# Crossbar turns of the first two mLSTM heads: the loads that turn them on ScalarE's queue, the head's norm ahead of the next scores

## The chip, the cores and the metric

The kernel runs on one core of a Trainium2 chip. The metric is device time in microseconds (us). The core's engines are named as the profile names them: PE (TensorE, matrix products), DVE (VectorE), ACT (ScalarE), POOL (GpSimd) and SP (SyncE, which here does nothing but issue DMAs). DMAs are issued by SP, POOL or ACT and carried out by 16 DMA engines that they share. Each engine takes its instructions in the order in which they were written out; an instruction that waits holds all that stand behind it on that engine.

## The reference, cut to what matters

A trunk of two layers over 256 latent tokens and 256 context tokens, width 1024. Layer 0 mixes tokens by an mLSTM with four heads, then comes a ConvFFN; layer 1 is a latent attention with eight heads, then a ConvFFN. The change lies in the mLSTM alone, whose heads are computed so:

```python
q, k = jnp.split(x_c @ w_qk, 2, axis=-1)          # per head: 256 columns of q, 256 of k
v = (x_m @ w_v)                                    # per head: 512 columns
wmat = jnp.exp(dmat - mj[..., None]) * jnp.einsum("bhjd,bhsd->bhjs", qc, kc)
num = ... + jnp.einsum("bhjs,bhse->bhje", wmat, vc)
h = num / jnp.maximum(jnp.abs(den), jnp.exp(-mj))[..., None]
...
o = jax.nn.sigmoid(h_in @ w_og)                    # output gate
hsum = o * s
return _head_rms_norm(hsum, norm_g) @ w_out        # a norm over each head's 512 columns
```

The kernel does not scan in chunks: for each head it forms the whole 512 x 512 matrix of decays and scores, for both directions.

## The kernel before, in words

**Products.** A product in fp32 is done as three matmuls on a high and a low part (`mm3`, L428: L431, L434, L435). `split` (L444) makes the two parts: a cast on ACT (L445) gives the high one, a subtraction on DVE (L446) the low one.

**Weights.** `Stream` brings weights in tiles of 128 x 1024 (512 KB, tile `raw`) on SP's queue (L309), three of them ahead. Each is split as well: the cast of `w` or `wu` on ACT (L346), the low part on DVE (L369). A `raw` tile is free for the next load when both have read it. One tile feeds 24 matmuls of 128 x 512.

**The loop over heads** (`build`, L2250 on). For each head h PE does, in this order: 192 matmuls `qk` (`w_qk`, 8 weight tiles), then for h of 1 and more the 36 matmuls `av` of the head before (`av`, L1169), then the 24 matmuls `sc` and `sl` of this head's scores (`s_mm`), which ACT copies to `S` (L1043). `w_qk` takes two steps of the background (`bg`) after each of its eight weight tiles, sixteen in all, and what a step writes stands on every engine at that place. Ahead of its seventh tile it calls `v_load` for the head before: loads of `vr` and `oh` on POOL (L1139, L1145) and the split of `v`.

**What is in the background of `w_qk(h)`.** `head(h-1)`: the decays `aB` are loaded on POOL (L1051) and masked on DVE (`Am`, L1056), the exponentials of `W` are made on ACT (L1093), `W` is multiplied by the scores, summed and divided on DVE (L1094 to L1111), turned on PE (`PT`, L1124: 12 matmuls of 128 x 128) and split. For h of 2 and 3 also `post(h-2)`, the norm of the head before that: sums of squares on ACT (`jk`, L1194), a root with a table load (L1195), a reciprocal and a scaling on DVE (L1196, L1198); that is its first step. Its second step turns the rows into two planes of 16 bits (`pl`, ACT, L450) and stores them to DRAM on POOL (`hd`, L1205). They come back turned by four loads through the DMA's crossbar (`turn_load`, L1246, DMA_TRANSPOSE, on SP's queue), and `turn_split` splits them to `hn` on ACT and DVE (L1254, L1255). `mixed` (L1225) deals these out over the sixteen steps by a string: `h` is a step of `head`, `p` one of `post`, `L` a turning load, `S` a `turn_split`, `.` nothing.

**Beside it** runs the modulation of later layers (`ada_bg`): 1.2-us products on DVE (`junk`, L550), each of which reads a one-element gate that ACT copies just before (`adav<-w` or `mod<-w`, L565); their loads `ar` are on SP (L573). POOL also prepares sums of weights for later (`t4d`, L1709).

**After the loop** come the matmuls `y` of the output projection, with `head(3)`, `post(2)` and the `v` of head 3 in the background; their `W` is turned by the same line L1124.

Of the kernel before, what the change touches and what calls it, by code (L numbers as in the profile page):

```python
# [10 lines left out]
U16 = mybir.dt.uint16  # L11
# [390 lines left out]
class K:  # L402
# [620 lines left out]
    def s_mm(self, h):  # L1023
# [10 lines left out]
        for jb in range(2):  # L1034
# [4 lines left out]
            pl.append(p)  # L1039
        S = []  # L1040
        for p in [pc] + pl:
            s = self.s2("S")
            nc.scalar.activation(s, p, AF.Copy, scale=1.0 / 16.0)  # L1043
            S.append(s)
        return S

    def head(self, h, S, big=False):
        nc = self.nc
# [13 lines left out]
        for g in range(3):  # L1062
# [9 lines left out]
            for i, t in enumerate(jbs):  # L1072
                base = 256 * i if g == 0 else 0
                for d in range(2):
# [17 lines left out]
                    for s0, s1, src in spans:  # L1092
                        nc.scalar.activation(o[:, base + s0:base + s1], src[:, s0:s1], AF.Exp, bias=bias, scale=1.0)  # L1093
                    nc.vector.scalar_tensor_tensor(o[:, base + lo:base + hi], o[:, base + lo:base + hi], 1.0,  # L1094
                                                   S[g][:, base + lo:base + hi], op0=ALU.mult, op1=ALU.mult,
                                                   accum_out=den[:, 2 * i + d:2 * i + d + 1])
# [127 lines left out]

    def mixed(self, head, post):  # L1225

        plan = "h p p hp h hL . L hL . hLS h S S . S"
        for step in plan.split():
            for op in step:
                if op in "hp":  # L1230
                    next(head if op == "h" else post, None)
                elif op == "L":
                    self.turn_load()
                elif op == "S":
                    self.turn_split()
            yield

    def turn_load(self):

        h, d, e = self.turned[0]  # L1240
        if e == 3:
            self.turned.pop(0)
        else:
            self.turned[0] = h, d, e + 1
        x = self.s2("hx")
        self.nc.sync.dma_start_transpose(x.bitcast(U16), d.rearrange("t h n -> (t h) n")[:, e * 128:(e + 1) * 128])  # L1246
        self.hx.append((h * 4 + e, x))

    def turn_split(self):
# [979 lines left out]
def build(tc, off, a, out):  # L2229
    es = ExitStack()  # L2230
    with es:
        k = K(tc, es, off, a)
# [14 lines left out]
        S = None  # L2247
        tt = None
        k.hn, k.turned, k.hx = {}, [], []
        for h in range(H0):  # L2250
            gens = []
            if h == 0:
                gens.append(k.gate_chain())
            if h >= 2:
                gens.append(k.mixed(k.head(h - 1, S), k.post(h - 2, tt)))
            elif h >= 1:
                gens.append(k.head(h - 1, S))
            k.bg = gens
            k.w_qk(h, 2, (lambda: k.v_load(h - 1)) if h >= 1 else None)
            k.drain()  # L2260
            if h >= 1:
                tt = k.av(h - 1)
            S = k.s_mm(h)
        k.xc = None
        hn = lambda i: (k.hn[i][:, 0], k.hn[i][:, 1])
# [7 lines left out]
        tt = k.av(3)  # L2273
# [136 lines left out]
```

## Time and profile before

| | us |
|---|---|
| three runs | 1359.21, 1360.93, 1361.62 (median 1360.93) |
| the profiled execution | 1360.79 |
| its span, from first to last instruction | 1359.0 |
| PE busy | 1337.2 |
| DVE busy | 1058.1 |
| ACT busy | 718.3 |
| POOL busy | 146.1 |

The span is what the trace shows; 1.79 us of the profiled execution lie around it. Busy time of PE is the time in which a matmul is in flight; its mean granted clock is 0.993 of full speed. In a timeline a row is an instruction or a run of equal ones: start, duration, engine, line, what it writes and reads, and in brackets how long the engine stood idle before it and whose end released it. Durations of matmuls overlap, so their cost is the distance from start to start, 0.227 us for a 128 x 512 one at full clock.

### The profile page before, as it was taken

To read this page: it belongs to the slowest core of one execution; us is meant where nothing else is said; L and a number is where in the kernel's file an instruction comes from. 1 tells how busy PE (TensorE), PEld (TensorE's weight loads), DVE (VectorE), ACT (ScalarE), POOL (GpSimd) and SP (SyncE) were. 2 spreads that over 40 slices of the span, in tenths; PEclk is the share of its full clock that TensorE was granted. 3 is DMA by queue.
4 is the path that set the end of the run, shared out by engine and by line. 5 is a ranking of instruction groups with operands and counts; after the bars stand their busy time and mean duration, and the time that the engine had idled before them with its cause. 6 is when DMAs were issued, how large, how long until landed. Compare 5 with 4: busy or idle time off the path is not lost.

```text
span 1359.0 us, 18747 instructions
## 1 busy us (share of the span) xinstructions
PE 1337.2 (98%) x6627; PEld 1120.7 (82%) x6627; DVE 1058.1 (78%) x1745; ACT 718.3 (53%) x1260; POOL 146.1 (11%) x244
## 2 busy tenths in 40 slices
PE   9999999999999999889999999999999999999997
PEld 5777888888888878768898888888888988988886
DVE  4798656677788578787979987857889888898873
ACT  4765443455734456365644343333566768566660
POOL 0222000011201011120002111112000002000100
PEclk9999999999999999889999999999999999999999
DMA  9988847789676386966728989967976537466760
GB/s 363 325 277 275 277 170 235 246 287 300 224 269 221 135 217 210 251 242 231 235 76 283 290 275 296 265 183 186 311 233 187 162 102 213 143 205 191 258 191 32
DMA packets 108975, 308.24 MB, mean 227 GB/s; under 512 B 20888, under 2 KB 33688, under 8 KB 108800
## 3 DMA queue, kind: packets, MB, share of 16 engines
q1 hardware_dynamic: 71440, 220.75, 48.9%
q0 software_dynamic: 26640, 68.84, 18.6%
q10 hardware_dynamic: 10800, 17.44, 3.7%
q8 instruction: 52, 0.85, 0.2%
q14 instruction: 43, 0.35, 0.1%
HBM read 272.21 MB, written 44.21 MB: 233 GB/s over the span
## 4 chain that ended last, share of the span: by engine, by line
PE 92%; DMA 3%; DVE 2%; SPq 1%; issue 1%; ACT 1%; DVEq 0%; ACTq 0%
PE fin L1550 8%; PE y L435 6%; PE y L434 6%; PE y L431 6%; PE tok L431 6%; PE tok L434 6%; PE tok L435 6%; PE fin L434 6%; PE fin L431 6%; PE fin L435 6%; PE qk L431 3%; PE qk L435 3%; PE qk L434 3%; DMA raw<-in_ws 3%; PE up L724 2%; PE up L431 1%
## 5 line engine op out<-in xcount | busy, mean ns | idle before, releaser
L369 DVE TENSOR_TENSOR w<-raw,w 128x1024 fp32r<-128x1024 f32 (+2 forms) x286 | 342.8, 1202 | 153.7 <-ACT w L346 153.2
L346 ACT CAST w<-raw 128x1024 fp32r<-128x1024 f32 (+2 forms) x286 | 296.2, 1037 | 299.7 <-PE tok L435 77.3
L550 DVE SCALAR_TENSOR_TENSOR junk<-ar,bc 128x1024 f32<-128x1024 f32 x128 | 155.8, 1217 | 5.4 <-DMA raw<-in_ws 2.1
L434 PE MATMUL fin<-h,w 128*128 128x512 f32 (+1 forms) x370 | 139.6, 377 | 0.0
L431 PE MATMUL fin<-h,w 128*128 128x512 f32 (+1 forms) x370 | 139.5, 377 | 0.0
L435 PE MATMUL fin<-h,w 128*128 128x512 f32 (+1 forms) x370 | 139.3, 377 | 0.0
L1550 PE MATMUL fin<-h,w 128*128 128x512 f32 (+1 forms) x636 | 111.1, 337 | 0.0
L1550 PEld LDWEIGHTS fin<-h,w 128*128 128x128 f32 x636 | 97.6, 190 | 13.2
L431 PE MATMUL qk<-xc,w 128*128 128x512 f32 x256 | 100.0, 391 | 0.0
L435 PE MATMUL qk<-xc,w 128*128 128x512 f32 x256 | 99.7, 390 | 0.0
L434 PE MATMUL qk<-xc,w 128*128 128x512 f32 x256 | 99.6, 389 | 0.0
L435 PEld LDWEIGHTS fin<-h,w 128*128 128x128 f32 x370 | 69.6, 188 | 12.9
L434 PEld LDWEIGHTS fin<-h,w 128*128 128x128 f32 x370 | 69.6, 188 | 12.8
L431 PEld LDWEIGHTS fin<-h,w 128*128 128x128 f32 x370 | 69.6, 188 | 12.7
L435 PEld LDWEIGHTS qk<-xc,w 128*128 128x128 f32 x256 | 48.0, 188 | 10.0
L431 PEld LDWEIGHTS qk<-xc,w 128*128 128x128 f32 x256 | 48.1, 188 | 9.9
L434 PEld LDWEIGHTS qk<-xc,w 128*128 128x128 f32 x256 | 48.1, 188 | 9.9
L431 PE MATMUL tok<-w,hT 128*128 128x512 f32 x128 | 49.9, 390 | 0.0
L434 PE MATMUL tok<-w,hT 128*128 128x512 f32 x128 | 49.8, 389 | 0.0
L435 PE MATMUL tok<-w,hT 128*128 128x512 f32 x128 | 49.8, 389 | 0.0
L741 ACT ACTIVATE fg<-fg 128x512 f32<-128x512 f32 (+1 forms) x44 | 23.1, 525 | 50.0 <-DVE fg L739 43.9
L369 DVE TENSOR_TENSOR wu<-raw,wu 128x1024 fp32r<-128x1024 f32 (+1 forms) x37 | 44.0, 1204 | 7.0 <-ACT wu L346 6.5
(490 smaller groups left out, 3139.1 us busy)
## 6 DMA issues: line engine op xcount, KB each, us to landing
raw<-in_ws SPq DMA_DIRECT2D x282, 512.0 KB, 4.6
ar<-in_adaT SPq DMA_DIRECT2D x80, 512.0 KB, 5.6
t4d<-in_ws POOLq DMA_DIRECT2D x20, 512.0 KB, 8.7
adaw<-in_ada SPq DMA_DIRECT2D x16, 512.0 KB, 8.2
zr<-fd ACTq DMA_DIRECT2D x33, 128.0 KB, 4.4
xmd<-xr POOLq DMA_DIRECT2D x16, 256.0 KB, 4.6
xcd<-cv POOLq DMA_DIRECT2D x16, 256.0 KB, 5.1
xs<-xmd POOLq DMA_DIRECT2D x16, 256.0 KB, 6.9
```

The source lines that it names most:

```text
L346: self.cast = k.nc.scalar.copy(h[:, :cols], src)
L369: i = self.k.nc.vector.tensor_sub(l[:, :n], src, h[:, :n])
L431: q = mm(out, w[0], x[0], start=start, stop=False, skip_group_check=on)
L434: mm(out, w[0], x[1], start=False, stop=False, skip_group_check=on)
L435: mm(out, w[1], x[0], start=False, stop=stop, skip_group_check=on)
L550: nc.vector.scalar_tensor_tensor(o, w, 1.0, self.bc[j], op0=ALU.mult, op1=ALU.mult, accum_out=col[:, k, j:j + 1])
L724: nc.tensor.matmul(ps[m], wk[i][:, c], hT[k][:, j], start=made[m] == 0, stop=made[m] == 23)
L741: nc.scalar.activation(tmp[:, :n], tmp[:, :n], AF.Silu)
L1550: self.nc.tensor.matmul(ps[:, 0:256] if x else ps, w[x][:, k * 128:(k + 1) * 128], h[:, 0:256] if x else h, start=i == 0 and not k0, stop= ...
```

## The change

Three edits, all in the mLSTM.

```diff
     def mixed(self, head, post):
 
-        plan = "h p p hp h hL . L hL . hLS h S S . S"
+        plan = "p hp h hL h hL . L hS L hS . S . S ."
...
-        self.nc.sync.dma_start_transpose(x.bitcast(U16), d.rearrange("t h n -> (t h) n")[:, e * 128:(e + 1) * 128])
+        self.nc.scalar.dma_start_transpose(x.bitcast(U16), d.rearrange("t h n -> (t h) n")[:, e * 128:(e + 1) * 128])
...
             if h >= 2:
-                gens.append(k.mixed(k.head(h - 1, S), k.post(h - 2, tt)))
+                gens.append(k.mixed(k.head(h - 1, S), post))
...
             if h >= 1:
                 tt = k.av(h - 1)
+                if h < 3:
+                    post = k.post(h - 1, tt)
+                    next(post)
             S = k.s_mm(h)
```

The turning loads go from SP's queue to ACT's. The norm of heads 0 and 1 is written right behind their `av`, ahead of the next scores, and no longer inside the next `w_qk`. The plan puts the planes and stores first, the steps of `head` at 2, 3, 4, 5, 6, 9 and 11 (before at 1, 4, 5, 6, 9, 11 and 12), the turning loads at 4, 6, 8 and 10 (before 6, 8, 9 and 11) and the splits of the turned tiles at 9, 11, 13 and 15 (before 11, 13, 14 and 16). On PE the 12 turns `PT` of heads 1 and 2 so stand behind 120 of the 192 `qk` matmuls where they stood behind 144. On POOL the stores `hd` and the loads `aB` change places: two `hd`, one `aB`, two `hd`, one `aB`, where both `aB` stood first; the `t4d` stand behind them in place of between.

The first place is ACT in the middle of the third head's `qk`. Before, its instructions from the last four exponentials of `W` up to the gate copies of the modulation are these:

```order
L1093 ACTIVATE W<-Am_3915,gcol 128x128
L1093 ACTIVATE W<-aB_3909,gcol 128x384
L1093 ACTIVATE W<-Am_3916,gcol 128x128
L1093 ACTIVATE W<-aB_3910,gcol 128x256
L346 CAST w<-raw 128x1024
L445 CAST qk<-qk 128x512
L346 CAST w<-raw 128x1024
L565 COPY adav<-w 1x1 x5
```

And now, with the turning loads among them (the first of the four stands three rows ahead of these, before the cast of `qk` and that of a weight tile):

```order
L1093 ACTIVATE W<-Am_3940,gcol 128x128
L1093 ACTIVATE W<-aB_3934,gcol 128x384
L1093 ACTIVATE W<-Am_3941,gcol 128x128
L1093 ACTIVATE W<-aB_3935,gcol 128x256
L1246 DMA_TRANSPOSE hx<-hd 128x1024
L346 CAST w<-raw 128x1024
L1246 DMA_TRANSPOSE hx<-hd 128x1024 x2
L565 COPY adav<-w 1x1 x3
L445 CAST qk<-qk 128x512
```

Three turning loads now stand between the last exponential and the gate copies that release the modulation's products on DVE.

The second place is DVE just then, at the end of the same head's `W`. Before, a part of a weight tile stands ahead of the last product of `W`, the one that `PT` reads:

```order
L1104 RECIPROCAL R<-R 128x2
L550 SCALAR_TENSOR_TENSOR junk,adav<-ar,bc 128x1024
L1109 TENSOR_SCALAR W<-W,R 128x512
L369 TENSOR_TENSOR w<-raw,w 128x1024
L1111 SCALAR_TENSOR_TENSOR W<-W,R 128x512
```

And now a product of the modulation does:

```order
L1104 RECIPROCAL R<-R 128x2
L1109 TENSOR_SCALAR W<-W,R 128x512
L550 SCALAR_TENSOR_TENSOR junk,adav<-ar,bc 128x1024
L1111 SCALAR_TENSOR_TENSOR W<-W,R 128x512
L446 TENSOR_TENSOR qk<-qk 128x512
```

That product reads a gate copy of L565, which stands behind the third and fourth turning load on ACT: the last row of `W` now comes after them.

The third place is ACT behind `PT`, ahead of the `av` of the same head. Before:

```order
L346 CAST w<-raw 128x1024
L445 CAST PT<-PT 128x512 x3
L1254 ACTIVATE hn<-hx,sm 128x512
L445 CAST qk<-qk 128x512
L445 CAST v<-vr 128x512 x4
L1254 ACTIVATE hn<-hx,sm 128x512 x3
L346 CAST w<-raw 128x1024
```

And now:

```order
L346 CAST w<-raw 128x1024
L445 CAST PT<-PT 128x512 x3
L1254 ACTIVATE hn<-hx,sm 128x512 x2
L565 COPY adav<-w 1x1
L445 CAST qk<-qk 128x512
L445 CAST v<-vr 128x512 x4
L346 CAST w<-raw 128x1024
```

The rows read alike, but `PT` now comes one weight tile earlier: the cast at the top of the first list and the one at the foot of the second are of the same weight tile (108 casts of L346 stand up to it in either program), and the casts of `PT` and `v` no longer stand behind it.

## The prediction

> **What bounds the kernel now.** The page first: PE is busy nearly the whole span.
>
> ```profile
> PE 1337.2 (98%) x6627; PEld 1120.7 (82%) x6627; DVE 1058.1 (78%) x1745; ACT 718.3 (53%) x1260; POOL 146.1 (11%) x244
> ```
>
> So the change, which adds and removes no matmul, can win only where PE waits or runs below its full clock. The waits of PE come next (what waited, for what, total, times, longest):
>
> ```profile
> PE PT L1124 <- DVE W L1111: 5.4, 1, 5.4
> PE av L431 <- ACT v L445: 2.7, 1, 2.7
> PE av L434 <- DVE v L446: 2.4, 2, 1.3
> ```
>
> All three are in the mLSTM. PE's timeline says what they cost, measured over whole stretches. The 36 `av` and 24 score matmuls run from the first `av` to the next first `qk` (head 0), the next first `qk` (head 1), and the first `y` (head 2):
>
> ```profile
> 446.71 0.39 PE L431 MATMUL av<-v,PT 128*128 128x512 f32 x1
> ...
> 459.05 0.39 PE L431 MATMUL qk<-xc,w 128*128 128x512 f32 x1
> ...
> 503.93 0.40 PE L431 MATMUL av<-v,PT 128*128 128x512 f32 x1
> ...
> 518.43 0.39 PE L431 MATMUL qk<-xc,w 128*128 128x512 f32 x1
> ...
> 563.07 0.39 PE L435 MATMUL qk<-xc,w 128*128 128x512 f32 x1
> 566.19 0.80 PE L431 MATMUL av<-v,PT 128*128 128x512 f32 x1 [2.74 <-ACT v L445]
> ...
> 582.43 0.39 PE L431 MATMUL y<-w,hn 128*128 128x512 f32 x1
> ...
> 592.18 0.39 PE L434 MATMUL y<-wu,hn 128*128 128x512 f32 x1
> 597.95 1.12 PE L1124 MATMUL PT<-ident,W 128*128 128x128 f32 x4 [5.38 <-DVE W L1111]
> ```
>
> Head 0 is undisturbed: 12.34 us (48 matmuls 512 wide at the pitch of 0.227 and 12 of `sc` at half of it would be 12.2). Head 1 takes 14.50, **2.16** more. Head 2 should start at 563.07 + 0.23 = 563.30 and takes 19.13, **6.79** more. The transposes of head 3 come at 597.95 where 592.18 + 0.23 = 592.41 was due, **5.54** late. Behind two of the three places the clock is down (windows: start and end, length, busy time and count of each engine, granted clock, DMA share, GB/s):
>
> ```profile
> 596.50:603.40 6.90, 5.45 (x15) 4.50 (x16) 6.90 (x23) 6.40 (x16) 0.00 (x0) 0.51 0.16 67
> 565.80:572.70 6.90, 5.46 (x12) 4.00 (x13) 6.90 (x12) 6.90 (x12) 1.07 (x2) 0.51 0.97 349
> ```
>
> The second lies in the 6.79 already. In the first, 5.45 us of work at 0.51 cost 5.45 x 0.49 = **2.7**. Together 2.16 + 6.79 + 5.54 + 2.7 = 17.2 us that can go.
>
> What released `v` so late? ACT's timeline for heads 1 and 2 and the chain of waits:
>
> ```profile
> 499.64 1.05 ACT L346 CAST w<-raw 128x1024 fp32r<-128x1024 f32 x1 [11.87 <-DMA raw<-in_ws]
> 500.60 1.56 ACT L445 CAST PT<-PT 128x512 fp32r<-128x512 f32 x3
> ...
> 503.12 2.20 ACT L445 CAST v<-vr 128x512 fp32r<-128x512 f32 x4
> ...
> 562.02 1.05 ACT L346 CAST w<-raw 128x1024 fp32r<-128x1024 f32 x1 [14.77 <-DMA raw<-in_ws]
> ...
> 565.49 2.20 ACT L445 CAST v<-vr 128x512 fp32r<-128x512 f32 x4
> ```
> ```profile
> 486.69 12.85 DMA raw<-in_ws
> ```
>
> ACT stood 11.87 and 14.77 us at a weight cast with `PT`, `qk` and `v` queued behind it. The load it waited for was issued at 486.69, behind turning loads on SP, and needed 12.85 us. SP's own timeline shows how long turning loads hold their issuer:
>
> ```profile
> 476.90 1.25 SPq L1246 DMA_TRANSPOSE hx<-hd  x1
> ...
> 480.36 6.23 SPq L1246 DMA_TRANSPOSE hx<-hd  x3
> ...
> 540.27 9.21 SPq L1246 DMA_TRANSPOSE hx<-hd  x3
> ```
>
> **The change part by part.** (1) *Turning loads off SP's queue.* For SP they go altogether: in that stretch it issues weight and modulation loads only. The load that went out at 486.69 can go out once its buffer is free, up to 6.2 us sooner, and its fellow a head later up to 9.2. I don't count on it landing sooner, though: the median from issue to landing in this stretch is that of a crowded bus, on queues that never had a turning load too:
>
> ```profile
> raw<-in_ws SPq DMA_DIRECT2D x6, 512.0 KB, 12.8
> ...
> vr<-vd POOLq DMA_DIRECT2D x4, 256.0 KB, 7.0
> oh<-od POOLq DMA_DIRECT2D x4, 256.0 KB, 11.8
> aB<-ad POOLq DMA_DIRECT2D x2, 256.0 KB, 5.1
> ```
>
> The Trainium skill speaks against this part: "DMA: Bandwidth & Descriptors", section "Issuing engines are not separate DMA queues", holds that issuing from several engines saves only the time of the issuing sequencer, since the same 16 DMA engines carry it all. The 7.0 and 11.8 us on POOL's queue agree with it; by that rule alone the weight would land as late as before, and the sum would stay at 1347 by part (2) or, without it, at 1361.
>
> (2) *The plan.* PT and the `v` casts move ahead of the cast that was late. Even if its load lands at 499.5 again, `v` no longer stands behind it. I estimate the `v` casts from `PT`: at 24 matmuls earlier, 491.69 (the row below) less 24 x 0.227 = 5.44, PE reaches `PT` at 486.25; three casts (1.56), two `hn`, one `qk` and four `v` (2.20) then end on ACT by about 496 (the estimate allows `hn` and `qk` as much as `v`), DVE's shares a microsecond later, against `av` due at 503.9. Some 6 us of slack: 2.16 and 6.79 go. The loads `vr` stand behind `W` in the old order and in the new, so they go out earlier with it.
>
> ```profile
> 491.69 1.47 PE L1124 MATMUL PT<-ident,W 128*128 128x128 f32 x12
> ```
>
> (3) *PT 5.44 us earlier* needs `W` that much earlier. Before, its last product ran at 490.15 (below), 15.6 us from the second batch of exponentials at 475.32 to its end at 490.89. That batch waited for the second table load, behind the planes:
>
> ```profile
> 470.11 3.89 ACT L450 COPY pl<-oh 128x1024 uint16<-128x1024 uint16 x4 [1.97 <-DVE oh L1198]
> 474.02 1.28 ACT L1093 ACT_TABLE_LOAD   x1
> 475.32 0.69 ACT L1093 ACTIVATE W<-Am,gcol 128x128 f32<-128x128 f32 x2
> ...
> 477.09 0.57 ACT L445 CAST qk<-qk 128x512 fp32r<-128x512 f32 x1
> ...
> 478.51 0.40 ACT L1093 ACTIVATE W<-Am,gcol 128x128 f32<-128x128 f32 x1
> ...
> 480.49 0.61 ACT L1093 ACTIVATE W<-aB,gcol 128x384 f32<-128x384 f32 x1
> ```
> ```profile
> 455.06 0.69 DVE L1184 TENSOR_TENSOR oh<-av,oh 128x512 f32<-128x512 f32 x1 [2.03 <-PE av L435]
> ...
> 469.59 1.68 DVE L1198 TENSOR_SCALAR oh<-oh,ss 128x512 f32<-128x512 f32 x4
> ...
> 490.15 0.74 DVE L1111 SCALAR_TENSOR_TENSOR W<-W,R 128x512 f32<-128x512 f32 x1
> ```
>
> *The norm first* moves all this: the outputs are complete at 455.75; the last square sum, a score copy, a table load (1.28) and the root end near 458.9 (estimated from the rows of the same kinds), the scaling (1.68) near 460.8, planes (3.89) 463.9. One weight cast and the second table load follow: the exponentials may start at 467.3, or once `aB`, now issued among and behind the stores at 463 to 465, has landed, 5.1 us later, by 470. I take the middle, 468.6, against 475.32. From there ACT needs 3.5 us for eleven exponentials (six took 1.77, from 475.32 to 477.09; five others are partly wider), 1.25 for the first turning load, 1.4 for the casts of `qk` and a weight (477.09 to 478.51), 1.5 for four exponentials, two of them wide (0.61): 7.6 in all.
>
> Now the new dependence: the last product of `W` stands behind a modulation product whose gate copy stands behind turning loads 2 to 4 on ACT. The trace of before has no turning load on ACT. Lower bound: 3 x 1.25 = 3.8 us, each as the single one on SP; upper bound: 9.2, the three at 540.27. I take the 6.2 at 480.36, which is the same stretch. With one cast (1.05), the modulation product (1.2) and the last product of `W` (0.74): 468.6 + 7.6 + 6.2 + 3.0 = **485.4**, against PE's arrival at 486.25: a slack of 0.9 us, with `aB` and the turning loads able to move it by 3 either way. I book 0.5 per head, 1.0 for the two.
>
> The norm ahead of the scores also delays ACT's `S` copies by about 1 us; the exponentials that follow start no earlier than 467.3, which hides it. The stores on POOL go earlier by the same 7 us, so the turning loads find their data.
>
> (4) *Head 3's PT*, 5.54 + 2.7. Its exponentials need `S`, which ACT copied behind a late weight, and DVE had no idle time from the stall at 562.02 to the first `y`:
>
> ```profile
> 584.55 1.05 ACT L346 CAST wu<-raw 128x1024 fp32r<-128x1024 f32 x1 [5.41 <-DMA raw<-in_ws]
> ```
> ```profile
> 563.10:582.40 19.30, 15.51 (x62) 12.24 (x61) 19.30 (x28) 11.15 (x20) 2.13 (x4) 0.82 0.84 287
> ```
>
> The scores end about 582.4 and `S` could follow only at 584.55 + 0.96 = 585.5, so without that wait it comes 3.1 us earlier; a mere shift leaves 5.5 - 3.1 = 2.4 late. DVE without its backlog may take the rest. Bounds: nothing stays, or all 8.2. I take 2.0 lost, clock included.
>
> **Sum:** 17.2 - 1.0 - 2.0 = 14.2. The profiled execution of 1360.79 becomes 1346.6; the median of the runs is 0.14 above it: **1347**.
>
> **The rivals.** *PT waits for W behind the turning loads on ScalarE.* If these hold ACT 9.2 us as at 540.27, `W` is ready at 488.4, a wait of 2.1 us, and a wait of 2.74 was followed by half clock at 566.19: another 2.7. Two heads lose 9.6; with the 1.0 booked taken out of the 1346.6, that is 1345.6 + 9.6 = 1355, and 1358 if `aB` lands at 470. For it: four loads in one queue behind each other, now beside SP's weight loads. Against: they are spread over six steps and find an empty queue.
>
> *Nothing gained: the loads move, the bus stays.* If the weights land as late and something else in the queue ahead of `v` waits for them (the cast just before `PT`, which now stands a tile earlier but whose `raw` may be a late one as well), the waits of `av` and of head 3 stay: about 1361. For it: 12.8 us for a load in this stretch. Against: the load ahead of that one was cast at 486.49 in time, and the late one now stands behind `v`. (The rule of the Trainium skill cited above would have the loads as late as this rival has them.)
>
> *Slower: the turning loads hold ACT longer than they held SP.* One mechanism, at the second to fourth of them. Beside it 17.2 - 2.0 = 15.2 us are won, so it decides when each head loses 7.6, a wait of 4.9 and 2.7 of clock: at a hold of 6.2 + 0.9 + 4.9 = 12.0 us. At twice the 9.2 of 540.27, 18.4, the wait would be 11.3, two heads would lose 28, and 1345.6 + 28 = 1374. For it: weight loads that stood still behind the turning loads now run against them on the same DMA engines. Against: nothing in the trace holds an issuer that long.
>
> **How the numbers follow.** Forecast 0.60, from 1343.5 (nothing given back) to 1349.5. PT waiting for W 0.18, 1350 to 1358. Nothing gained 0.10. Slower 0.12. A measurement of this kernel tells about 0.2%, 2.7 us, from no change: faster 0.78, same 0.10, slower 0.12. The range runs from 1343 to 1360: it holds the forecast, the first rival and a little of the second.
>
> **What would show it right or wrong.** Right: no `av` row with a wait; SP's weight loads go out without gaps while ACT shows four DMA_TRANSPOSE of 1 to 3 us; `PT` of heads 1 and 2 unwaited or under a microsecond; the wait at head 3 below 2 us with full clock. Wrong in (3): a wait of PT for W in heads 1 and 2 and half clock behind it. Wrong in (2): ACT idle for `raw` ahead of `PT`. Wrong in all: turning loads of more than 4 us each on ACT.

## The result and the profile after

| | before | after |
|---|---|---|
| first runs, median (lowest to highest), us | 1361.18 (1359.21 to 1361.62, 4 runs) | 1347.49 (1344.9 to 1349.55, 4 runs) |
| ratio to before, 95% interval | | 0.9901 [0.9878, 0.9924] |
| the profiled execution, us | 1360.79 | 1349.55 |
| its span, us | 1359.0 | 1347.8 |

The kernel became faster by 13.7 us, 1.0%. Five more runs of the changed kernel, made later beside the last experiments, had a median of 1344.72 (1343.19 to 1348.15).

The waits of PE after, in the same view as before (what waited, for what, total, times, longest); both waits of `av` are gone; of `PT` one is left and a small one has come (the second row stood there before, too):

```profile
PE PT L1124 <- DVE W L1111: 4.6, 2, 4.2
PE idle L661 <- DVE adav L503: 1.5, 1, 1.5
```

PE's timeline at the same places, the `av` and score stretches of heads 1 and 2 and `PT` of heads 2 and 3:

```profile
503.67 0.39 PE L431 MATMUL av<-v,PT 128*128 128x512 f32 x1
...
516.01 0.39 PE L431 MATMUL qk<-xc,w 128*128 128x512 f32 x1
...
544.25 0.52 PE L1124 MATMUL PT<-ident,W 128*128 128x128 f32 x3 [0.41 <-DVE W L1111]
...
561.51 0.39 PE L431 MATMUL av<-v,PT 128*128 128x512 f32 x1
...
573.86 0.39 PE L431 MATMUL y<-w,hn 128*128 128x512 f32 x1
...
582.01 0.39 PE L431 MATMUL y<-wu,hn 128*128 128x512 f32 x1
586.59 1.12 PE L1124 MATMUL PT<-ident,W 128*128 128x128 f32 x4 [4.19 <-DVE W L1111]
```

Head 1 now takes 516.01 - 503.67 = 12.34 us and head 2 takes 12.35, as head 0 did before: the 2.16 and 6.79 are won whole. `PT` of head 3 comes at 586.59 where 582.01 + 0.23 = 582.24 was due: still 4.35 late, against 5.54. Behind it the clock is down for a shorter time than before (windows; busy time of PE 3.21, granted clock 0.55):

```profile
586.00:589.80 3.80, 3.21 (x10) 2.73 (x11) 3.77 (x15) 3.80 (x8) 0.00 (x0) 0.55 0.48 189
```

That costs 3.21 x 0.45 = 1.4 in place of 2.7. The balance of this execution: 2.16 + 6.79 + (5.54 - 4.35) + (2.7 - 1.4) - 0.41 = 11.0 us, of 1359.0 - 1347.8 = 11.2.

ACT's timeline in head 1's stretch holds the first surprise. `ACTq` is the part of ACT that issues; `ACT` the part that computes:

```profile
471.51 0.40 ACT L1093 ACTIVATE W<-Am,gcol 128x128 f32<-128x128 f32 x1 [4.00 <-DVE Am L1056]
471.67 1.47 ACTq L1246 DMA_TRANSPOSE hx<-hd  x1
...
473.28 0.50 ACT L1093 ACTIVATE W<-aB,gcol 128x256 f32<-128x256 f32 x1
473.35 2.57 ACTq L1246 DMA_TRANSPOSE hx<-hd  x1
473.68 0.39 ACT L1093 ACTIVATE W<-Am,gcol 128x128 f32<-128x128 f32 x1
...
476.03 1.25 ACTq L1246 DMA_TRANSPOSE hx<-hd  x1
...
477.37 1.26 ACTq L1246 DMA_TRANSPOSE hx<-hd  x1
477.59 1.03 ACT L346 CAST w<-raw 128x1024 fp32r<-128x1024 f32 x1
478.68 0.38 ACT L565 COPY adav<-w 1x1 f32<-1x1 f32 x3
```

The issue at 473.35 takes 2.57 us, and exponentials and casts that stand ahead of it in the program run meanwhile without a gap: a turning load is issued while the work written ahead of it is still being computed. It holds only what stands behind it, and only when that earlier work runs out first. The same in head 2's stretch:

```profile
533.65 5.64 ACTq L1246 DMA_TRANSPOSE hx<-hd  x1
533.91 0.56 ACT L445 CAST qk<-qk 128x512 fp32r<-128x512 f32 x1
...
539.39 1.26 ACTq L1246 DMA_TRANSPOSE hx<-hd  x1
540.69 0.38 ACT L565 COPY mod<-w 1x1 f32<-1x1 f32 x3 [2.83 <-DVE R L1100]
```

Of an issue of 5.64 us and one of 1.26, ACT stood idle 2.83 (the releaser named, a DVE instruction, is not what the copy stood behind: it runs as the last issue ends).

The second surprise is in the issues (KB each, median us from issue to landing), in the stretch where a weight took 12.8, `oh` 11.8 and a turning load 14.5 us before:

```profile
raw<-in_ws SPq DMA_DIRECT2D x8, 512.0 KB, 6.7
...
vr<-vd POOLq DMA_DIRECT2D x4, 256.0 KB, 5.4
oh<-od POOLq DMA_DIRECT2D x4, 256.0 KB, 7.5
hx<-hd ACTq DMA_TRANSPOSE x4, 6.6
```

All of these land sooner, the weights in about half the time, and the weight cast that had waited 11.87 us runs at 495.56 without a wait. The prediction had not counted on that. Which of the three edits did it?

### The profile page after: what moved, and what is told of

It is laid out like the page before. It is cut to its first block, busy times and chain, and to the rows that moved or that the text cites. A ratio compares the mean times of both kernels' runs of the same rounds, so it can differ in the third digit from the quotient of the medians.

```text
span 1347.8 us, 18731 instructions
## 1 busy us (share of the span) xinstructions
PE 1332.8 (99%) x6627; PEld 1118.6 (83%) x6627; DVE 1059.7 (79%) x1745; ACT 719.8 (53%) x1260; POOL 146.7 (11%) x244
## 4 chain that ended last, share of the span: by engine, by line
PE 82%; issue 10%; DVE 4%; DMA 2%; POOL 1%; ACT 1%; DVEq 0%; SPq 0%; POOLq 0%; ACTq 0%
PE fin L1550 8%; PE y L434 6%; PE y L435 6%; PE y L431 6%; PE tok L431 6%; PE tok L434 6%; PE tok L435 6%; PE fin L434 6%; PE fin L431 6%; PE fin L435 6%; PE up L724 2%; PE up L431 1%; PE up L434 1%; PE up L435 1%; PE y L1393 1%
## 5 line engine op out<-in xcount | busy, mean ns | idle before, releaser
L346 ACT CAST w<-raw 128x1024 fp32r<-128x1024 f32 (+2 forms) x286 | 296.2, 1037 | 273.8 <-PE tok L435 82.1
L434 PEld LDWEIGHTS fin<-h,w 128*128 128x128 f32 x370 | 69.7, 188 | 12.8
```

Of the source, the lines that this page charges most:

```text
L346: self.cast = k.nc.scalar.copy(h[:, :cols], src)
L434: mm(out, w[0], x[1], start=False, stop=False, skip_group_check=on)
```

## The experiments

The runs of each group below were compared with before on the same chip (its medians: 1361.26, 1361.72, 1359.95 and 1361.42).

| run | what it is | median, us | ratio to before, 95% interval |
|---|---|---|---|
| e1 | queue alone | 1372.51 | 1.0070 [1.0045, 1.0095] |
| e2 | plan and norm, no queue | 1346.87 | 0.9906 [0.9883, 0.9928] |
| e3 | queue and plan, no norm | 1349.15 | 0.9909 [0.9887, 0.9930] |
| e4 | queue and norm, no plan | 1374.64 | 1.0106 [1.0087, 1.0125] |
| e5 | plan alone | 1355.61 | 0.9959 [0.9941, 0.9976] |
| e6 | head's steps alone | 1348.19 | 0.9896 [0.9877, 0.9916] |
| e7 | norm, stores, turning loads early | 1349.27 | 0.9904 [0.9881, 0.9927] |
| e8 | before with plain loads | 1345.54 | 0.9883 [0.9865, 0.9900] |
| e9 | change, masks of head 3 early | 1349.78 | 0.9923 [0.9907, 0.9939] |
| e10 | e9 on SP's queue | 1349.52 | 0.9931 [0.9915, 0.9948] |
| e11 | the change again | 1344.72 | 0.9891 [0.9875, 0.9907] |
| e12 | e4 without the fourth turning load | 1350.45 | 0.9911 [0.9880, 0.9940] |

### Each edit undone, and the queue alone (e1 to e4)

Three candidates stood at the start. Theory A, the prediction's: `v` stood behind a late weight cast, and the plan moved it ahead. Theory B: SP was held in turning loads, so the queue did it. And for the norm: PT needs its early start.

e1, before with one line changed:

```diff
-        self.nc.sync.dma_start_transpose(x.bitcast(U16), ...
+        self.nc.scalar.dma_start_transpose(x.bitcast(U16), ...
```

> Before with the turning loads on ScalarE's queue alone; old plan, norm inside the next qk. Theory A (order): what cost the 9 us at av was that v stood behind a late weight cast; the load lands late in any case, since the DMA engines are crowded, so the waits of av stay for the most part: 1355 to 1361 us. Theory B (SP's hold): the cast was late only because SP stood 6.2 and 9.2 us in turning loads; without them its loads go out in time, the waits of av go and the time falls to about 1347 to 1351, as with the whole change.

Measured 1372.51 (1357.92 to 1377.63, 12 runs): slower by 0.7%. Neither theory had that. ACT's timeline and the issues of that run, in head 1's stretch:

```profile
506.89 1.04 ACT L346 CAST w<-raw 128x1024 fp32r<-128x1024 f32 x1 [19.19 <-DMA raw<-in_ws]
```
```profile
raw<-in_ws SPq DMA_DIRECT2D x6, 512.0 KB, 12.7
...
oh<-od POOLq DMA_DIRECT2D x4, 256.0 KB, 23.6
hx<-hd ACTq DMA_TRANSPOSE x4, 18.5
```

The weight that `v` stands behind is later still than before (19.19 us of wait against 11.87), and `oh` takes twice as long. SP issues no turning load any more and it did not help: B falls. Nor is it a held ACT: the longest of its issues takes 4.55 us, and the cast waits for the load. The suspicion that is left: the loads slow each other.

e2, the change with that line undone:

> The change with the turning loads back on SP's queue; new plan, norm first. Theory A (order): v no longer stands behind the late cast, so av does not wait although the weight still lands late: 1347 to 1351. Theory B (SP's hold): SP is held as before, the weights behind are late, the stall only moves to PT or to the first products of the next head: 1354 to 1361.

1346.87: as the whole change. With the new plan and the norm first the queue is worth nothing that these runs can tell.

e3, the change without the norm first:

```diff
-                gens.append(k.mixed(k.head(h - 1, S), post))
+                gens.append(k.mixed(k.head(h - 1, S), k.post(h - 2, tt)))
...
-                if h < 3:
-                    post = k.post(h - 1, tt)
-                    next(post)
```

> The change without the norm first: queue and new plan, the norm back at step 1 of the next qk. By the prediction's step 3 the exponentials start some 4 to 7 us later while PT stays 24 matmuls early: PT of heads 1 and 2 waits 3 to 5 us for W each, with half clock behind it: 1355 to 1362. Rival: the chain was set by the landing of aB and not by the norm (in the profile of the change the exponentials stood 4.0 and 4.8 us for Am), so little changes: 1346 to 1351.

1349.15, and in its profile `PT` of heads 1 and 2 does not wait at all: the expectation failed and the time is the rival's. The chain of `W` does not hang on the norm here: the exponentials start behind the planes and the table load at 470.57, without waiting for `aB`, where those of the change wait for `aB` until 471.51. What the norm first wins, the later `aB` takes back.

e4, the change with the plan of before:

```diff
-        plan = "p hp h hL h hL . L hS L hS . S . S ."
+        plan = "h p p hp h hL . L hL . hLS h S S . S"
```

> The change with the old plan: queue and norm first, PT 24 matmuls later, turning loads at steps 6, 8, 9 and 11. Theory A (order): v again stands behind the cast that was late, waits of av in part: 1351 to 1358. Theory B (SP's hold): loads go out in time, so no wait of av: 1346 to 1350.

1374.64, slower than before by 1.1%. This is the prediction's slower rival, in the other plan. ACT's timeline, with the issues of the fourth turning load of both heads:

```profile
478.18 10.45 ACTq L1246 DMA_TRANSPOSE hx<-hd  x1
488.67 0.28 ACT L565 COPY adav<-w 1x1 f32<-1x1 f32 x2 [10.38 <-issue]
...
551.30 17.50 ACTq L1246 DMA_TRANSPOSE hx<-hd  x1
568.84 0.28 ACT L565 COPY mod<-w 1x1 f32<-1x1 f32 x2 [17.43 <-issue]
```

Here the work ahead had run out, and ACT stood 10.38 and 17.43 us in one issue ("issue": it waited for nothing else that the profile shows), with a weight cast, `PT` and `v` behind it. In head 2 PE waits for that: the weight cast behind the hold runs at 569.51, and `qk` stands 7.29 us for it. In head 1 the hold was over in time (`v` was cast on ACT at 498.01). There `av` stands 11.63 us for DVE's part of `v`, which is behind modulation products, and these wait for late loads: one for its own `ar`, one for a gate copy that stands on ACT behind the late fourth tile `hx`.

```profile
499.95 1.23 DVE L550 SCALAR_TENSOR_TENSOR junk<-ar,bc 128x1024 f32<-128x1024 f32 x1 [3.50 <-DMA ar<-in_adaT]
505.56 0.72 ACT L1254 ACTIVATE hn<-hx,sm 128x512 fp32r<-128x512 f32 x1 [4.12 <-DMA hx<-hd]
508.25 1.23 DVE L550 SCALAR_TENSOR_TENSOR junk<-ar,bc 128x1024 f32<-128x1024 f32 x1 [5.79 <-ACT adav L565]
514.33 0.80 PE L434 MATMUL av<-v,PT 128*128 128x512 f32 x1 [11.63 <-DVE v L446]
...
570.60 0.80 PE L431 MATMUL qk<-xc,w 128*128 128x512 f32 x1 [7.29 <-ACT w L346]
```

So the plan carries the gain in these four, and decides whether the queue is harmless.

### The plan taken apart (e5 to e8)

Theory C, collision: turning loads that run beside the loads of `vr` and `oh` make all of them slow. The plan could then help by its order (A) or by keeping the two apart (C).

e5, before with the plan's line alone:

> Before with the new plan alone (turning loads on SP, norm inside the next qk). After the first four runs: the plan carries the whole gain, queue and norm nothing. Expected 1345 to 1351 like the change. Rival: the norm first and the queue each hide the other's absence, and one of them is needed: 1353 or more.

1355.61 (1350.56 to 1359.8, 9 runs): less than half of the gain. A weight cast still waits for its load, now ahead of `PT`:

```profile
492.36 1.05 ACT L346 CAST w<-raw 128x1024 fp32r<-128x1024 f32 x1 [10.63 <-DMA raw<-in_ws]
...
553.96 1.05 ACT L346 CAST w<-raw 128x1024 fp32r<-128x1024 f32 x1 [14.28 <-DMA raw<-in_ws]
```

These waits are nearly as long as before (11.87 and 14.77). The `av` and score stretch of head 1 runs from 502.81 to 515.96 and that of head 2 from 561.44 to 579.27, still 0.81 and 5.49 more than 12.34: order alone wins 2.7 of the 9.0 us.

The norm first is worth nothing with the queue (e3) and some 7 to 9 us without it (e2 against e5, by the ratios and by the medians). In the same way the queue is worth nothing with the norm first (e2) and some 6 to 7 us without it (e3 against e5). The norm alone was not run. Why the two cover for each other is not settled; in e5 the turning loads went out at 472.84, when `vr` followed at 475.00.

e6, before with head's steps alone moved:

```diff
-        plan = "h p p hp h hL . L hL . hLS h S S . S"
+        plan = ". hp hp hp h hL . L hL . hLS . S S . S"
```

> Before with only the steps of head moved, to those of the change (2, 3, 4, 5, 6, 9, 11), so that the casts of PT and v stand ahead of the late weight cast; norm, planes, stores and turning loads where they were, on SP. Theory A (order): that suffices, 1345 to 1351. Theory C (collision): the turning loads still run at the same time as the loads of vr and oh (POOL) and both take long, weights behind them are late, the stall moves to another place: 1354 to 1365.

1348.19: the whole gain, as A says, and not the 1354 to 1365 of C. But its weights land in 4.8 us (median), so the time does not show what order alone is worth. Nor does it fit C as it was put: `vr` went out at 476.84 in place of 480.88, behind the earlier `W`, with the turning loads on SP beside it from the start,

```profile
476.45 2.58 SPq L1246 DMA_TRANSPOSE hx<-hd  x2
...
479.76 8.60 SPq L1246 DMA_TRANSPOSE hx<-hd  x2
```

and still `vr` landed in 5.5 us and `oh` in 7.7 (before: 7.0 and 11.8).

e7, e2 with this plan:

```diff
-        plan = "p hp h hL h hL . L hS L hS . S . S ."
+        plan = "ph p . hL h hL . L hS L hS h S . S ."
```

> The change with the turning loads on SP and the steps of head back at 1, 4, 5, 6, 9, 11 and 12; norm first, planes, stores and turning loads early. Theory A (order): v stands behind the late cast again, waits of av: 1354 to 1361. Theory C (collision): the turning loads are through before vr and oh start, no load is late, no wait of av: 1345 to 1351.

1349.27: the whole gain again, with `v` behind a weight cast as before. In head 1 that cast came at 493.07 after a wait of 5.77 us, `v` at 496.55, in time. In head 2 it was later and only just in time (`av` waited 0.5 us), but 6.4 us sooner than the 562.02 of before:

```profile
555.61 1.05 ACT L346 CAST w<-raw 128x1024 fp32r<-128x1024 f32 x1 [10.99 <-DMA raw<-in_ws]
```

So the new order of head's steps is not needed; the norm, stores and turning loads early do as well.

e8, before with plain loads in place of the crossbar's:

```diff
-        self.nc.sync.dma_start_transpose(x.bitcast(U16), d.rearrange("t h n -> (t h) n")[:, e * 128:(e + 1) * 128])
+        self.nc.sync.dma_start(x.bitcast(U16), d.rearrange("t h n -> t (h n)")[e * 128:(e + 1) * 128, :])
...
-        i = self.nc.scalar.copy(dst, src.bitcast(U16).rearrange("p (n h) -> p h n", h=2))
+        i = self.nc.scalar.copy(dst.rearrange("p h n -> p (h n)"), src.bitcast(U16))
```

> Before with the four turning loads of each head as plain loads of the same 256 KB, on the same queue at the same place, and the planes copied without being taken apart, so that the heads 0 and 1 are not turned. Theory C (collision): it is the many small pieces of the crossbar loads that crowd out the others; as plain loads they take a few us, SP is not held, the weight is in time, no wait of av: 1345 to 1352. Theory A without C: SP's order and the bytes are the same, the weight behind is late by about as much: 1356 to 1361.

1345.54 (1345.08 to 1347.8), with the plan, queue and order of before. The issues in the same stretch:

```profile
raw<-in_ws SPq DMA_DIRECT2D x8, 512.0 KB, 5.1
hx<-hd SPq DMA_DIRECT2D x4, 256.0 KB, 5.9
...
oh<-od POOLq DMA_DIRECT2D x4, 256.0 KB, 6.3
```

The same bytes at the same place, without the crossbar: the weight cast ahead of `v` still waits, but 4.77 us in place of 11.87, and no `av` waits:

```profile
492.13 1.05 ACT L346 CAST w<-raw 128x1024 fp32r<-128x1024 f32 x1 [4.77 <-DMA raw<-in_ws]
```

Plain loads also hold SP less (each issue 0.33 to 0.42 us), but that lets the weight out only 2.4 us sooner, at 484.30 in place of 486.69, and its cast comes 7.5 us sooner. So what cost the 9 us before is that these loads go through the crossbar: beside them the others land late, and C holds so far. (In that stretch 4576 DMA packets were under 512 B before and 496 are in e8; whether it is the number of packets or the crossbar itself was not separated.)

That the two kinds of load must be kept apart in time is not shown, and the change does not do it: when its `vr` goes out at 476.77, 2675 of the 4224 packets of head 1's turning loads still have to pass. What the kernels with the gain share in head 1 is that the weights land sooner: in 4.8 to 7.3 us (median; 9.1 in e10), against 9.4 to 12.8 in before, e1, e4 and e5. `vr` and `oh` need not: they took 8.5 and 11.1 in e7. In head 2 the medians of the weights do not sort them (17.1 in e3, which has the gain, 6.8 in e5). Why either way of moving the steps makes the weights land sooner is not settled.

A's share is small as long as the weights stay late: that is e5, with 2.7 of the 9.0 us. (In e10 the casts ahead of `PT` wait 7.82 and 11.23 us, and no `av` waits.)

### The rest: PT of head 3 (e9 to e11)

The exponentials of head 3 waited 3.08 us for the masks `Am`, which stood behind modulation products. e9 writes head 3's first step ahead of its scores:

```diff
+                if h == 3:
+                    S3 = []
+                    head3 = k.head(3, S3, True)
+                    next(head3)
             S = k.s_mm(h)
+        S3.extend(S)
...
-        k.bg = [k.head(3, S, True), k.post(2, tt, True)]
+        k.bg = [head3, k.post(2, tt, True)]
```

> The change, and the first step of head 3 (loads of aB, masks Am) written ahead of its scores in place of behind them, so that on VectorE the masks no longer stand behind modulation products. In the profile of the change PT of head 3 waits 4.2 us and the exponentials wait 3.1 us for Am. Theory D: that wait, with the half clock behind it, is the whole difference between the change's runs near 1345 and those near 1349. Expected 1343 to 1346, with less spread. Rival: the copies of S behind late weight casts on ScalarE set it; then the wait stays and so does the time, 1345 to 1350.

1349.78 (1348.35 to 1353.43): no gain; the change itself had 1344.72 on the same chip (e11). The rival held. In its profile `S` waits behind a weight, longer than in the change:

```profile
576.49 1.05 ACT L346 CAST wu<-raw 128x1024 fp32r<-128x1024 f32 x1 [7.88 <-DMA raw<-in_ws]
...
578.63 0.58 ACT L1043 ACTIVATE S<-sc 128x512 f32<-128x512 f32 x1
```

e10 is e9 with the turning loads on SP:

> The same with the turning loads on SP's queue. Since the queue made no difference with the new plan (1346.87 against 1347.49), the same as the run before: 1343 to 1346. Rival: on ScalarE's queue the turning loads free SP and gain a little when nothing else is left to wait for: 1 to 3 us slower than the run before.

1349.52: the same as e9, so again no difference by queue.

e11 is the change itself:

> The change itself on the same chip as the two before, for the comparison with them. 1345 to 1350, in two groups as in its first four runs (1344.9 and 1346.0, 1349.0 and 1349.6); a profile near 1349 shows a wait of PT at head 3 of 4 us or more, one near 1345 a wait below 2 us.

1344.72, with one of five runs at 1348.15. The profile is of a run of 1344.74; the other was of one of 1349.55. The wait of `PT` is shorter:

```profile
PE PT L1124 <- DVE W L1111: 1.8, 2, 1.4
```

1.4 us of wait at head 3 against 4.2, and no half clock behind it. Its copy of `S` starts at 572.20 where the other's starts at 576.00. Between runs of one and the same program this wait, set by when the weights ahead of `S` land, makes most of the difference of 4.8 us: 4.2 - 1.4 = 2.8 of wait, and 1.4 of clock. In this profile the weights of head 1 land in 6.8 us as in the other, but `vr` and `oh` take 7.2 and 10.4, nearly as long as before.

### What a held issuer costs (e12)

e12 is e4 with the fourth turning load of each head left out and the third's tile read in its place:

```diff
-        x = self.s2("hx")
-        self.nc.scalar.dma_start_transpose(...
+        if e < 3:
+            x = self.turned_last = self.s2("hx")
+            self.nc.scalar.dma_start_transpose(...
+        x = self.turned_last
```

> The run with the old plan (queue and norm of the change) without the fourth turning load of each head; the last quarter of heads 0 and 1 is taken from the tile of the third, so their output is not the reference's. In the profile with all four, the fourth's issue held ScalarE 10.5 and 17.5 us while the third's packets were on their way. Theory F (held issuer): a turning load's issue on ScalarE lasts until the one before it is through, and what costs the 13 us over before is that ScalarE stands there; without the fourth nothing stands behind the slow third: 1345 to 1353. Rival (crowded engines alone): three turning loads beside the loads of vr and oh are late nearly as four are, and so are the weights: 1358 to 1371.

1350.45 (1347.44, 1348.29, 1352.6 and 1360.18). In the median the 24 us between e4 and this hang on one load in four. The profile is of the run at 1360.18, and there a hold and a late weight both show:

```profile
479.51 0.38 ACT L565 COPY adav<-w 1x1 f32<-1x1 f32 x3 [3.37 <-issue]
...
497.00 1.05 ACT L346 CAST w<-raw 128x1024 fp32r<-128x1024 f32 x1 [10.21 <-DMA raw<-in_ws]
```

ACT is held 3.37 us and no longer 10.38, but a weight is 10.21 us late. So most of e4's loss goes with the fourth load. But leaving it out takes away its long hold, its late landing and a quarter of the crossbar's traffic together, and in e4's own profile the hold made PE wait in head 2 and late loads in head 1. How much of the 24 us is the hold is not shown. Late loads without the long hold still cost one run of four.

## Why the prediction was right, and where not

**The size** was right: 1347 forecast, 1347.49 measured in the first runs, 1344.9 as the median of all nine.

**The 2.16 and 6.79 at `av`** were won whole, but not for the reason given. That was order, and in the change's own profile it had little to do: the cast that `v` no longer stands behind ran without a wait in both heads (495.56 and 553.40). Nor is order enough when the weights stay late: in e5 the late cast stands ahead of `PT`, the sign named for "wrong in (2)", and 0.81 and 5.49 of the 2.16 and 6.79 stay. So the step "even if its load lands at 499.5 again" does not carry the forecast, and luck made up for it: against "I don't count on it landing sooner" the weights did land sooner, in head 1 in 6.7 us against 12.8. It is the crossbar loads that had made them late (e8), and moving the turning loads early, together with norm and stores, is one way to have them sooner (e7, 6.0 us); why it helps is open.

**The queue**, by the rule of the Trainium skill ("DMA: Bandwidth & Descriptors", "Issuing engines are not separate DMA queues"), saves only issue time. With the new plan and the norm first the runs agree: nothing between e2 and the change, nothing between e9 and e10. Elsewhere they don't: moving the same loads to another engine cost some 10 us in the old plan (e1, 0.7%) and won some 6 to 7 in the new one without the norm first (e3 against e5), so there "only save the time" is too little said.

**PT early, W early.** The end of `W` was forecast at 485.4 and came at 484.8 (its last product ran at 484.05), a wait of 0 and 0.41 us against 1.0 booked. That it fits so well is luck: terms of that sum were wrong and cancelled. All exponentials but the first started at 471.51, not at 468.6, since the second mask waited for `aB`:

```profile
470.78 0.69 DVE L1056 TENSOR_TENSOR Am<-aB,mask 128x512 f32<-128x512 f32 x1 [1.64 <-DMA aB<-ad]
...
484.05 0.75 DVE L1111 SCALAR_TENSOR_TENSOR W<-W,R 128x512 f32<-128x512 f32 x1
```

From there to the end of `W` it took 13.3 us, where 7.6 + 6.2 + 3.0 = 16.8 were booked. The turning loads, booked in it as 1.25 and 6.2 us of ACT's time, held the gate copies for none of it in head 1 and for 2.83 in head 2: their issue runs beside the work written ahead of them. What set the end of `W` was DVE, busy for 13.78 of the 14.02 us from 470.78 to 484.80. Nor did `PT` need the norm first (e3). A slip besides: 463.9 + 1.05 + 1.28 is 466.2 and not 467.3; the first exponential ran at 467.10.

**Head 3** is the term that was mis-sized: 2.0 booked, 4.35 + 1.4 lost in the profiled run, 1.5 in the other profile. The step's mechanism, `S` behind a weight cast, was right (e9); that the weight would be in time was not always so:

```profile
568.71 1.05 ACT L346 CAST wu<-raw 128x1024 fp32r<-128x1024 f32 x1 [4.22 <-DMA raw<-in_ws]
...
571.87 1.05 ACT L346 CAST wu<-raw 128x1024 fp32r<-128x1024 f32 x1 [2.02 <-DMA raw<-in_ws]
...
576.00 0.58 ACT L1043 ACTIVATE S<-sc 128x512 f32<-128x512 f32 x1
```

**The rivals.** "Slower, the turning loads hold ACT" was a true mechanism at the wrong plan: it forecast 1374 at holds of 18.4 us in each head, and e4, with holds of 2.62 + 10.38 = 13.0 and 3.97 + 17.43 = 21.4, measured 1374.64. That the number fits is partly luck, for PE then waited behind the hold in one head alone, at `qk` and not at `PT` as the rival has it, and behind late loads in the other. In the change the holds were 0 and 2.83, so the milder rival, `PT` behind the turning loads, came to 0.41 us. "Nothing gained" fell with the landing times; its mechanism, a late weight just ahead of `PT`, is what e5 shows.

No version tried beats the change by more than these runs can tell; e8, which does not turn the heads, marks what is left to win here: about nothing.

## What to carry to other kernels

When an engine idles at a load, look at what else is on the DMA engines in the same microseconds before reordering the waiters: here four crossbar loads of 256 KB more than doubled the landing time of the weights (12.8 us against 5.1 with plain loads), and issuing them some 7 us sooner, with the norm and stores that feed them (e7), was worth as much as reordering the waiters. Here a crossbar load did no harm where its issuer had a stock of work written ahead of it (0 and 2.83 us), and did where it had none (e4, head 2). And test edits that come together one at a time and in pairs: of the three here the plan alone won less than half, with either of the others the whole, and the queue alone was a loss.

## What the runs showed of the hardware that was not expected

- ACT issued a DMA while computing what was written ahead of it (an issue of 5.64 us from 533.65, casts and exponentials without a gap until 537.8). It stood still only for what was left of the issue after that.
- The issue of a crossbar load is not constant: in head 1 of e4 the four took 1.26, 1.18, 2.82 and 10.45 us, in head 2 up to 17.50. The first two found no packets of another on the way; the last stood while those of the second and third passed beside `vr`, `oh` and weights. But in e3 all eight took 1.18 to 1.29 us, so what sets it is open.
- The same four loads cost the same on either queue with the new plan and the norm first, and some 10 us more on ACT's queue with the old plan (e1); the cause below the level of landing times (which engine, which port) was not looked into and stays open.
